# A hybrid decoder step on one core: the eight buffers of four moving rows get places at multiples of 512 bytes

## Chip, core and metric

The kernel runs on one core of a Trainium2 chip. The metric is the device time of one execution in microseconds (us); lower is better. The text speaks of TensorE (the matrix engine, PE in the profile, with PEld for its weight loads), VectorE (DVE), ScalarE (ACT), GpSimd (POOL) and the DMA queue of SyncE (SP). SBUF is the on-chip memory in which an operand's row lies in each of 128 partitions, PSUM the one that TensorE writes.

## What is computed

One decoder layer, for a prompt of 256 tokens and 8 samples of 4 tokens (288 tokens together), D = 2048, feed-forward width 8192, all in float32:

```python
h = rms_norm(x, norm1)
z = h @ w_in                       # all projections at once
q, k = partial_rope(...)           # sliding-window attention, 16 heads, sinks
o_swa, swa_state = swa_fn(q, k, v, sink)
log_a = log_sigmoid(ag @ w_a2 + b_a) / 16
o_g, S_new = gla_recurrent(q_g * 256**-0.5, k_g, v_g, log_a, S0)   # 4 heads, 256 x 512 states
o_g = rms_norm_per_head(o_g) * silu(rg)
y = sigmoid(gs) * (o_swa @ p_swa) + sigmoid(gg) * (o_g @ p_gla)
x = x + y @ w_o
h2 = rms_norm(x, norm2)
x = x + square(relu(h2 @ w_up)) @ w_down
```

Outputs are the final norm of x, the attention caches and the recurrent states.

## The kernel before

Activations lie transposed: a *row* k is one tile of 128 features by 288 tokens, so D = 2048 makes 16 rows. Every large product runs through `gemm` (L231): it streams one group of weights, 512 output features wide, in chunks (L234). A chunk is 512 KB of weights for two rows of k; ScalarE copies each half to `whi` (L227) and VectorE writes the rest of the precision to `wlo` (L228). For each row k and each of four slices m of 128 output features, three matmuls follow one another into the same bank of PSUM (L257 to L261): `whi` with the row's high part, `whi` with its low part, `wlo` with its high part. The weights are the stationary operand, the row of 288 columns is the moving one. A chunk has 2 x 4 x 3 = 24 matmuls, a gemm of 8 chunks has 192, and the 520 chunks have 12,480. At the end of a gemm the four banks are read out by `evac`, and the next gemm needs them empty again, bank after bank (`pmm` has four of them).

The order of the gemms is written out by hand (`ORDER`, L78): input projections (kv, q, gs, qk, v, gg, rg) with the attention projections ps among them, then pg0 to pg3, wo0 to wo3, and four blocks of up (four gemms) and dn (four gemms). Up to rg1 the attention and the linear attention are slipped between the chunks (`pump`, L211), with small matmuls of their own. From rg1 on TensorE runs gemm after gemm, up to the last one (dn3_3), with nothing between; VectorE does the states of the samples beside them (L1055).

The rows of a gemm come from these tiles. `rows` (L188) makes tiles of n rows that are 320 columns apart (1280 bytes), of which 288 are used; tiles whose name begins with hl, yl, ul, gl or h2l, all low parts, start 16 columns (64 bytes) into their buffer:

- `hh`, `yh`, `uh` (buffer XH) and `hl`, `yl`, `ul` (buffer XL): 16 rows each, for the input projections, wo and dn.
- eight buffers of four rows, Za0 to Za3 and Zb0 to Zb3, 5120 bytes each. For pg, row k is row k % 4 of `gh[k // 4]` and `gl[k // 4]`: gh0 to gh3 lie in Za0, Za2, Za3, Za1 (L991), gl0 to gl3 in Zb0 to Zb3 (L1013). For up, `h2h[j]` lies in Za j and `h2l[j]` in Zb j (L1034, L1035). So rows 12 to 15, that is chunks 6 and 7 of each of these gemms, use Zb3 for the low part, in pg beside Za1 and in up beside Za3.
- earlier the same eight buffers hold other tiles of the attention and linear attention, among them `kx1` (Zb3), `pt` and `kc` (Zb2, Za3), `e` (Za2, Za3), and at the end `kept` (all eight), which small matmuls read.

A pool gives each named buffer (tag) its place when a tile of that name is first asked for, one behind another, each as large as the largest tile of that name. XH, XL, Za2, Za1 and Zb1, the ten buffers of `whi` and `wlo`, come out at multiples of 512 bytes. Then come rs_m, the small nf, YA, zr and tt, and behind them Zb3, rs_t, Zb2, Za3, Za0, Zb0, sr, acc and rso.

Of the kernel before, what the change touches and what calls it, by code (L numbers as in the profile page):

```python
# [12 lines left out]
F32 = mybir.dt.float32  # L13
F32R = mybir.dt.float32r
# [5 lines left out]
P = 128  # L20
# [122 lines left out]
def step_kernel(ctx: ExitStack, tc: tile.TileContext, a: dict):  # L143
    nc = tc.nc
    V, S, G, T, SY = nc.vector, nc.scalar, nc.gpsimd, nc.tensor, nc.sync
    main = ctx.enter_context(tc.tile_pool(name="main", bufs=1))
# [38 lines left out]
    def big(tag, name, dt=F32, n=KT):  # L185
        return main.tile([P, n, NT], dt, name=name, tag=tag)

    def rows(tag, name, n=KT):  # L188

        off = 16 * name.startswith(("hl", "yl", "ul", "gl", "h2l"))  # L190
        return main.tile([P, n, 320], F32R, name=name, tag=tag)[:, :, off:off + NT]
# [116 lines left out]

    xa = big("SG", "x")
    hh, hl = rows("XH", "hh"), rows("XL", "hl")  # L310
    xn = []

    def x_row(k):
# [939 lines left out]
def build(arrays):  # L1253
    nc = bacc.Bacc("TRN2", target_bir_lowering=False, num_devices=1)
    aps = {}
    for n, v in arrays.items():
        aps[n] = nc.dram_tensor(f"in_{n}", v.shape, mybir.dt.from_np(v.dtype), kind="ExternalInput").ap()
    for n, s in OUTS.items():
        aps[n] = nc.dram_tensor(f"out_{n}", s, F32, kind="ExternalOutput").ap()
    with tile.TileContext(nc) as tc:  # L1260
        step_kernel(tc, aps)
    return nc
# [22 lines left out]
```

## Time and profile before

| | us |
|---|---|
| median of 3 runs | 1727.1 |
| lowest and highest of the runs | 1720.6 and 1727.28 |
| the profiled execution | 1727.3 |
| its span, first to last instruction | 1725.6 |
| TensorE busy in it | 1718.5 |
| VectorE busy | 1231.2 |
| ScalarE busy | 885.0 |

All times of the trace below are of the profiled execution, in us from the start of its span. The profile gives a matmul a duration that reaches into the next ones, because matmuls are pipelined; how long TensorE takes for each is read from the distance of their starts, or from the time that a stretch with a known number of them takes.

### The profile page before, as it was taken

The page shows a single profiled execution, that of the slowest core. Times are in us where ns is not written, and L with a number is a line of the kernel's source. Part 1 is how long each engine was busy: PE and PEld are TensorE (multiplying, and loading weights), DVE is VectorE, ACT ScalarE, POOL GpSimd, SP SyncE. Part 2 cuts the span into 40 slices and gives each one's busy share as a digit, 9 for nine tenths or more (in the row PEclk, how much of TensorE's full clock was granted, in tenths as well). Part 3 has the DMA queues.
Part 4 walks back from the last instruction along what each step waited for, and adds up shares of the span by engine and source line. Part 5 has one row for each costly group of instructions (what it writes and reads, how often), then busy time and mean ns, then how long its engine had stood idle before and what let it go on. Part 6 is the DMA issues. An engine that isn't in the chain of part 4 may idle for free.

```text
span 1725.6 us, 34513 instructions
## 1 busy us (share of the span) xinstructions
PE 1718.5 (100%) x13331; PEld 1691.6 (98%) x13331; DVE 1231.2 (71%) x2408; ACT 885.0 (51%) x1679; POOL 3.1 (0%) x12
## 2 busy tenths in 40 slices
PE   9999999999999999999999999999999999999998
PEld 8999999999999999999999999999999999999998
DVE  8885676857757576666778777677777777767554
ACT  7675464534544555544555554455445554445543
POOL 0000000000000000000000000000000000000000
PEclk9999999999999999999999999999999999999999
DMA  8778576676775655547657777866777687676753
GB/s 296 213 221 287 183 224 252 198 239 208 225 255 187 208 196 184 178 159 279 221 207 263 261 244 272 279 227 238 281 262 259 217 276 277 240 267 222 258 165 117
DMA packets 131701, 398.81 MB, mean 231 GB/s; under 512 B 21360, under 2 KB 39728, under 8 KB 127440
## 3 DMA queue, kind: packets, MB, share of 16 engines
q1 hardware_dynamic: 130096, 393.98, 67.2%
q10 hardware_dynamic: 1440, 2.62, 0.4%
q8 instruction: 104, 1.70, 0.4%
q14 instruction: 61, 0.50, 0.1%
HBM read 360.73 MB, written 35.82 MB: 230 GB/s over the span
## 4 chain that ended last, share of the span: by engine, by line
PE 99%; DMA 0%; DVE 0%; ACT 0%; issue 0%
PE mm L260 95%; PE pos L914 1%; PE mm L1180 1%; PE score L477 0%; PE o L520 0%; PE po L839 0%; DMA raw<-in_w 0%; PE po L842 0%; PE pa L767 0%; PE os L602 0%; PE scs L563 0%; PE ag L372 0%; PE po L841 0%; PE ssq L269 0%; PE pa L780 0%; PE pa L775 0%
## 5 line engine op out<-in xcount | busy, mean ns | idle before, releaser
L227 ACT CAST whi<-raw 128x512 fp32r<-128x512 f32 x1040 | 630.5, 618 | 714.4 <-PE mm L260 640.6
L167 DVE TENSOR_TENSOR wlo<-raw,whi 128x512 fp32r<-128x512 f32 x1040 | 702.3, 687 | 406.8 <-ACT whi L227 402.8
L260 PE MATMUL mm<-hh,whi 128*128 128x288 f32 x1472 | 433.9, 296 | 0.2 <-ACT whi L227 0.2
L260 PE MATMUL mm<-hl,whi 128*128 128x288 f32 x1472 | 431.2, 294 | 0.0
L260 PE MATMUL mm<-hh,wlo 128*128 128x288 f32 x1472 | 429.1, 292 | 0.0
L260 PE MATMUL mm<-h2l,whi 128*128 128x288 f32 x1024 | 302.2, 295 | 0.0
L260 PE MATMUL mm<-h2h,whi 128*128 128x288 f32 x1024 | 301.4, 294 | 0.0
L260 PE MATMUL mm<-h2h,wlo 128*128 128x288 f32 x1024 | 301.2, 294 | 0.0
L260 PE MATMUL mm<-uh,whi 128*128 128x288 f32 x1024 | 301.1, 294 | 0.0
L260 PE MATMUL mm<-ul,whi 128*128 128x288 f32 x1024 | 301.1, 294 | 0.0
L260 PE MATMUL mm<-uh,wlo 128*128 128x288 f32 x1024 | 300.7, 294 | 0.0
L260 PEld LDWEIGHTS mm<-hh,whi 128*128 128x128 f32 x1472 | 276.1, 188 | 6.5 <-ACT whi L227 3.7
L260 PEld LDWEIGHTS mm<-hh,wlo 128*128 128x128 f32 x1472 | 276.0, 188 | 0.1
L260 PEld LDWEIGHTS mm<-hl,whi 128*128 128x128 f32 x1472 | 275.9, 188 | 0.0
L260 PEld LDWEIGHTS mm<-h2h,wlo 128*128 128x128 f32 x1024 | 193.4, 189 | 0.0
L260 PEld LDWEIGHTS mm<-uh,wlo 128*128 128x128 f32 x1024 | 193.2, 189 | 0.0
L260 PEld LDWEIGHTS mm<-uh,whi 128*128 128x128 f32 x1024 | 192.4, 188 | 0.0
L260 PEld LDWEIGHTS mm<-h2h,whi 128*128 128x128 f32 x1024 | 192.4, 188 | 0.0
L260 PEld LDWEIGHTS mm<-h2l,whi 128*128 128x128 f32 x1024 | 191.9, 187 | 0.0
L260 PEld LDWEIGHTS mm<-ul,whi 128*128 128x128 f32 x1024 | 191.8, 187 | 0.0
L1073 DVE SCALAR_TENSOR_TENSOR acc_s<-vb,kdk,acc_s 128x512 f32<-128x512 f32 x192 | 142.4, 745 | 0.3
L260 PE MATMUL mm<-yl,whi 128*128 128x288 f32 x256 | 75.1, 294 | 0.0
(260 smaller groups left out, 1740.6 us busy)
## 6 DMA issues: line engine op xcount, KB each, us to landing
raw<-in_w SPq DMA_DIRECT2D x518, 512.0 KB, 4.3
vb<-vd SPq DMA_DIRECT2D x32, 1024.0 KB, 6.7
raw<-in_s SPq DMA_DIRECT2D x32, 512.0 KB, 4.6
old<-in_s SPq DMA_DIRECT2D x32, 512.0 KB, 4.9
out_ssn<-old SPq DMA_DIRECT2D x32, 512.0 KB, 4.6
pd<-tb SPq DMA_DIRECT2D x32, 96.0 KB, 2.1
pt<-pd SPq DMA_DIRECT2D x8, 384.0 KB, 4.7
kept<-kept SPq DMA_DIRECT2D x6, 512.0 KB, 5.9
```

The costliest lines, as they stand in the source:

```text
L167: eng.tensor_tensor(out, x, y, ALU.subtract)
L227: S.copy(hi, raw)
L260: T.matmul(o, lhsT=(lo if j == 2 else hi)[:, sl], rhs=xl(k) if j == 1 else xh(k), start=k == 0 and j == 0, stop=k == nk - 1 and j == 2)
L914: T.matmul(pos[r:r + 32], lhsT=qm[:, t, 32 * b:32 * b + 32], rhs=st[i + g][:, 512 * t:512 * t + 512], start=b < 2, stop=b >= NB - 2)
L1073: paced(V.scalar_tensor_tensor(acc[t], v(n), k(n), acc[t], ALU.mult, ALU.add))
L1180: mm = T.matmul(pst, lhsT=k[:, blk, P * t:P * t + P], rhs=v[:, blk], start=i == 0, stop=i == 5)
```

## The change

Right behind `hh` and `hl` a loop asks the pool for one tile of each of ten names, which nothing writes or reads. The sizes are those that the names have anyway.

```diff
     xa = big("SG", "x")
     hh, hl = rows("XH", "hh"), rows("XL", "hl")
+    for tag in ("Za2", "Za1", "Zb1", "whi", "wlo", "Zb3", "Zb2", "Za3", "Za0", "Zb0"):
+        if tag[0] == "Z":
+            main.tile([P, 4, 320], F32, name="place", tag=tag)
+        else:
+            main.tile([P, 512], F32R, name="place", tag=tag, bufs=5)
+
     xn = []
```

The order of places becomes Za2, Za1, Zb1, whi, wlo (as before), and then Zb3, Zb2, Za3, Za0, Zb0, ahead of rs_m. What each place is past a multiple of 512 bytes, worked out from the sizes in that order:

| buffer | before | after | its rows' starts before, past a multiple of 512 | after |
|---|---|---|---|---|
| Za1, Za2 | 0 | 0 | 0, 256, 0, 256 | the same |
| Zb1 (low part, 64 further on) | 0 | 0 | 64, 320, 64, 320 | the same |
| Za0, Za3 | 256 | 0 | 256, 0, 256, 0 | 0, 256, 0, 256 |
| Zb0, Zb2 (low part) | 256 | 0 | 320, 64, 320, 64 | 64, 320, 64, 320 |
| Zb3 (low part) | 128 | 0 | 192, 448, 192, 448 | 64, 320, 64, 320 |

rs_m, nf, YA, zr, tt and rs_t move by whole multiples of 512 bytes; all else in the pool, and the other pools, stay where they are, since the sum of the sizes is the same.

## Rows read from the trace of the kernel before

**Rows 1.** The page: span, TensorE's busy time (share, instructions), and the last chain by engine.
```profile
span 1725.6 us, 34513 instructions
...
PE 1718.5 (100%) x13331; PEld 1691.6 (98%) x13331; DVE 1231.2 (71%) x2408; ACT 885.0 (51%) x1679; POOL 3.1 (0%) x12
...
PE 99%; DMA 0%; DVE 0%; ACT 0%; issue 0%
```
**Rows 2.** Who TensorE waited for, whole span: us in total, times, longest.
```profile
PE mm L260 <- ACT whi L227: 0.2, 1, 0.2
PE ssq L269 <- DVE acc L164: 0.2, 1, 0.2
```
**Rows 3.** L260 by groups: busy us, mean ns of one, idle before.
```profile
L260 PE MATMUL mm<-h2l,whi 128*128 128x288 f32 x1024 | 302.2, 295 | 0.0
L260 PE MATMUL mm<-ul,whi 128*128 128x288 f32 x1024 | 301.1, 294 | 0.0
```
**Rows 4.** L260 by stretches, a gemm each: gg3, pg2, wo3, up0_1, dn0_1; window, length, busy, clock.
```profile
558.63:583.94 25.31, 25.31 (x194) 1.00 0.60 182
...
743.90:769.07 25.17, 25.17 (x195) 1.00 0.52 168
...
869.76:894.94 25.18, 25.18 (x195) 1.00 0.62 211
...
920.37:945.81 25.44, 25.44 (x195) 1.00 0.81 283
...
1022.00:1047.32 25.32, 25.32 (x194) 1.00 0.75 251
```
**Rows 5.** Timeline, TensorE: first matmul of each chunk of up0_1 and of up0_2's first.
```profile
920.37 0.29 PE L260 MATMUL mm<-h2h,whi 128*128 128x288 f32 x1
...
923.53 0.29 PE L260 MATMUL mm<-h2h,whi 128*128 128x288 f32 x1
...
926.69 0.30 PE L260 MATMUL mm<-h2h,whi 128*128 128x288 f32 x1
...
929.86 0.29 PE L260 MATMUL mm<-h2h,whi 128*128 128x288 f32 x1
...
933.03 0.29 PE L260 MATMUL mm<-h2h,whi 128*128 128x288 f32 x1
...
936.19 0.30 PE L260 MATMUL mm<-h2h,whi 128*128 128x288 f32 x1
...
939.35 0.29 PE L260 MATMUL mm<-h2h,whi 128*128 128x288 f32 x1
...
942.58 0.29 PE L260 MATMUL mm<-h2h,whi 128*128 128x288 f32 x1
...
945.81 0.29 PE L260 MATMUL mm<-h2h,whi 128*128 128x288 f32 x1
```
**Rows 6.** The same for chunks 6 and 7 of pg2 and the first of pg3.
```profile
762.78 0.29 PE L260 MATMUL mm<-gh,whi 128*128 128x288 f32 x1
...
765.92 0.29 PE L260 MATMUL mm<-gh,whi 128*128 128x288 f32 x1
...
769.07 0.29 PE L260 MATMUL mm<-gh,whi 128*128 128x288 f32 x1
```
**Rows 7.** Timeline where wo2 meets wo3, and wo3 meets up0_0: banks read out; up0_0's thirteenth matmul.
```profile
870.61 0.81 DVE L164 TENSOR_TENSOR x<-mm,x 128x288 f32<-128x288 f32 x2
...
895.89 0.81 DVE L164 TENSOR_TENSOR x<-mm,x 128x288 f32<-128x288 f32 x2
...
896.51 0.29 PE L260 MATMUL mm<-h2h,whi 128*128 128x288 f32 x1
```
**Rows 8.** Groups by line and shape: small matmuls that read the moved buffers.
```profile
L477 PE MATMUL score<-kx,qx 128*128 128x256 f32 x32 | 7.2, 306 | 0.0
...
L477 PE MATMUL score<-kx,qx 128*128 128x128 f32 x32 | 5.4, 249 | 0.0
...
L1180 PE MATMUL mm<-kept 128*128 128x512 f32 x24 | 5.9, 401 | 0.0
```

## Prediction

> **What bounds the kernel now.** I read the page first, then who TensorE waited for, then the pace of its matmuls, gemm by gemm and chunk by chunk. The page settles the engine: TensorE is busy for 1718.5 of 1725.6 us and 99% of the last chain is its own work [rows 1]. The waits show that it waits for almost nobody: two entries of 0.2 us [rows 2]. So no earlier transfer and no faster copy can bring time; only the pace at which matmuls follow one another can, and it is the only thing that a new place in SBUF could touch. The mean durations don't show that pace (294 and 295 ns for groups that differ in it, because durations overlap [rows 3]). Stretches of exactly one gemm, 192 matmuls, do: pg2 and wo3 take 25.17 and 25.18 us, dn0_1 25.32, up0_1 25.44 [rows 4], that is 131.1, 131.9 and 132.5 ns a matmul, all at the full granted clock (1.00). Two different things lie in these three figures.
>
> The first is a **rhythm**. pg2 and wo3 run at 25.17, dn0_1 at 25.32, although wo and dn read the same two buffers, XH and XL. gg3, on these buffers too, takes 25.31 [rows 4]. So the longer rhythm of dn, 0.14 to 0.15 us a gemm more, is no matter of where the rows lie; TensorE falls into it and stays. I went through the 12,480 starts in order of time: from the middle of rg1 to the end of wo3 every chunk has the short rhythm, and from up0_0 to the end every one the long.
>
> The second is **place**. Inside up0_1 the chunks begin at 920.37, 923.53, 926.69, 929.86, 933.03, 936.19, 939.35, 942.58 and 945.81 [rows 5]: the first six take 18.98 us together, 3.163 each, the last two 3.23 each. These two are rows 12 to 15, the only ones with the low part in Zb3, whose rows start 192 or 448 bytes past a multiple of 512. Chunks 0, 1, 4 and 5 use buffers at 256 past (Za0, Zb0, Zb2), chunks 2 and 3 buffers at 0, and they don't differ: 3.16 to 3.17 all. So an odd 256 costs nothing, the odd 128 of Zb3 0.067 us a chunk, 2.8 ns a matmul. All sixteen up gemms show the same jump at chunk 6.
>
> **The change, part by part.** (1) *The tiles named place* are not written or read: no instruction, no DMA, no wait is added or moved, on SP's queue or any other. The ring of five `whi` and five `wlo` buffers may start one further on; all ten lie at multiples of 512 bytes and each gemm uses all of them. Cost 0.
>
> (2) *Zb3 moves from 128 past to 0*, its rows to 64 and 320 past, which is where the rows of XL, Zb0, Zb1 and Zb2 start. I expect chunks 6 and 7 of an up gemm to take 3.163 us as chunks 0 to 5 do. The sum: 2 chunks x 0.067 us x 16 gemms = 2.1 us [rows 5]. The other way to it: up0_1 against dn0_1 in the same rhythm, 25.44 - 25.32 = 0.12 us, x 16 = 1.9 us [rows 4]. I take 2.0 us. All of it is on the path, because TensorE has nothing else in these stretches and the wait list has no L260 entry there [rows 2]. What is late next is nothing: VectorE and ScalarE have room (71% and 51% busy [rows 1]), and 2.0 us spread over 700 asks nothing more of them.
>
> (3) *pg reads Zb3 as well*, chunks 6 and 7 of four gemms. There it costs nothing now: pg2's chunks 6 and 7 take 3.14 and 3.15 us [rows 6], as an average chunk at 25.17 / 8 = 3.146 does. Nothing is to be gained. This is the one row that speaks against a plain rule "128 past costs": either the price is due in the long rhythm alone, or it needs the high part of Za3 beside Zb3, where pg has Za1. In both readings up's chunks 6 and 7 become like the others, because after the change Za3 and Zb3 lie as Za1 and Zb1 do.
>
> (4) *Za0, Za3, Zb0 and Zb2 move from 256 to 0.* By rows 5 that is worth 0.
>
> (5) *Small matmuls that read moved buffers.* `kx1` in Zb3 is the moving operand of half the 64 score matmuls, and `kept` is read by 24 matmuls and, with other tiles, 12 more at the end [rows 8]. Priced at what Zb3 costs a gemm's matmul, 2.8 ns, for 32 + 36 of them: 0.2 us at most, either sign; I take 0.
>
> (6) *rs_m, nf, YA, zr, tt and rs_t* move by whole multiples of 512, for VectorE, ScalarE and the DMA queues. The trace has no row of a duration that hangs on such a move; between wo (VectorE adds into x1, YA idle for it) and dn (states from YA) the matmuls' pace shows nothing of these engines beside the rhythm. 0.
>
> Sum: the profiled execution's 1727.3 - 2.0 = 1725.3 us. That execution stands 0.2 us above the median of the runs shown, so against the median the result would be 1725.1; I give 1725.3.
>
> [...]
>
> **Rivals.** *A, the long rhythm isn't entered.* It begins within up0_0, and one place there is tight. VectorE reads out banks 2 and 3 of wo3 from 895.89 on, 0.81 us for both; up0_0's thirteenth matmul, the first into bank 2, starts at 896.51, some 0.2 us behind the end of the first of the two. One gemm earlier the pair starts at 870.61, and the matmul that needs the bank follows at 869.76 + 12 x 0.131 = 871.33, some 0.1 us more room [rows 4, 7]. I read it so that the bank came a few ns late and that this slip threw TensorE from one rhythm into the other. If the slip fails to come, 32 gemms take 25.17 instead of 25.32, 0.14 to 0.15 us each, 4.6 us, and the 2.0 us of Zb3 are saved too: 1727.3 - 6.6 = 1720.7. The lowest run shown, 1720.6, is just there, so it seems to happen to the kernel as it is: by pg, the short rhythm has no price for Zb3, so that without the slip the old place and the new give the same 1720.7. For A: nothing in the margin is wide, and the change could set another beat upstream. Against: the order of VectorE's work is the same, and the median of the runs is that of a slip. Chance 0.22.
>
> *B, the change doesn't do what it says*: the price hangs on something that stays, such as which buffers pair up or what the last two chunks do besides. Against it: dn's last chunks have the same order and loads without the jump (its whole gemm, 25.32, is eight chunks of 3.165). 1727.3, chance 0.06. [...]
>
> *C, slower: the long rhythm rules earlier.* What decides is how TensorE comes out of the last of the slipped-in matmuls, in rg0 and rg1 near 618 us. Before, it came out short and stayed so for some eleven gemms up to 894.94. If it comes out long, these cost 11 x 0.14 = 1.5 us and leave a gain of 0.5. If the gemms before that, where breaks come every few chunks, run long as well, all the 33 gemms' worth ahead of up0_0 cost up to 33 x 0.14 = 4.6 us: 1725.3 + 4.6 = 1729.9. It is slower than before once more than 2.0 / 0.14 = 14 of them do. For it: gg3 shows that the long rhythm occurs there [rows 4]. Against: the breaks reset it, and nothing that the change moves decides it. Chance 0.08.
>
> **How the numbers follow.** Forecast 0.62 (1725.3, own range 1724.6 to 1726.0 from the two sums and the 0.2 us of the small matmuls), A 0.22 (1720.7), B 0.06 (1727.3), C 0.08 (1726.8 to 1729.9), 0.02 for what I don't see. A range for 8 in 10 has to reach from A to B; with 0.9 us below A and 0.7 above B for what separate executions differ by, 1719.8 to 1728.0. A difference under 0.5%, 8.6 us, can't be told from no change in a measurement of this kernel. No case reaches that: A is 0.38% faster, C at most 0.15% slower. So within 0.5%: 0.94, and 0.03 to each side for an unseen cause.
>
> **What would show it.** Right: in the up gemms all chunk distances are 3.16 to 3.17 us, an up gemm takes 25.31 to 25.33 us in the long rhythm (or 25.17 in the short), no longer 25.44; pg stays at 25.17; no new wait of L260. Wrong: chunks 6 and 7 still at 3.23 (B); a different distance in chunks 0, 1, 4 or 5, which would mean that an odd 256 matters after all. A shows as 25.17 in up and dn; C as 25.31 in rg2 to wo3. The forecast would fail in sign only if gemms ahead of up0_0 turned long for the most part, or if something that is not in these rows gave TensorE a new wait.

## The result

| | before | after |
|---|---|---|
| median of 20 runs each, us | 1727.0 | 1720.9 |
| lowest and highest | 1720.4 and 1727.6 | 1720.5 and 1725.4 |
| profiled execution (its span) | 1727.3 (1725.6) | 1720.8 (1719.0) |

The ratio of after to before is 0.9974, 95% interval 0.9965 to 0.9982 (it goes by all the single times, like the ratio of their means; the two medians stand at 0.9965). So after is faster, by less than 0.5%. The measured time lies 4.4 us below the forecast of 1725.3; it is that of rival A, 1720.7.

The medians hide what the single times show. Those of before lie in two groups with nothing between: 16 of 20 around 1727.1 (1726.7 to 1727.6) and 4 around 1720.8. Those of after lie in two groups as well: 18 of 20 around 1720.9 and 2 at 1725.0 and 1725.4. Every profiled execution in this study whose time is in a lower group runs up and dn in the short rhythm, every one in an upper group in the long one (or, in one kernel, in a variant of it). So I call the groups by the rhythm from here on, also where there is only a time.

The page of after, the lines that answer to [rows 1], and all that TensorE waited for, as in [rows 2]:

```profile
span 1719.0 us, 34513 instructions
...
PE 1711.6 (100%) x13331; PEld 1684.8 (98%) x13331; DVE 1230.4 (72%) x2408; ACT 884.5 (51%) x1679; POOL 3.1 (0%) x12
...
PE warm L405 <- DVE warm L399: 1.1, 1, 1.1
PE mm L260 <- ACT whi L227: 0.5, 1, 0.5
PE ssq L269 <- DVE acc L164: 0.2, 1, 0.2
```

The first of these waits, at the start of the kernel, is in before as well (1.1 us), though [rows 2] leave it out. The instructions are the same in number, TensorE is busy throughout as before, and there is no new wait. The span is 6.6 us shorter and TensorE's busy time 6.9 us (the wait for `whi` grew from 0.2 to 0.5 us): the gain is its pace alone. Stretches of one gemm in after (gg3, pg2, wo3, up0_0, up0_1, dn0_1, dn3_1; window, length, TensorE busy with its count, clock), against [rows 4]:

```profile
558.59:583.90 25.31, 25.31 (x194) 1.00 0.60 180
743.87:769.04 25.17, 25.17 (x195) 1.00 0.50 168
869.73:894.90 25.17, 25.17 (x194) 1.00 0.61 210
894.90:920.08 25.18, 25.18 (x194) 1.00 0.59 209
920.08:945.26 25.18, 25.18 (x195) 1.00 0.82 294
1020.78:1045.95 25.17, 25.17 (x194) 1.00 0.72 252
1624.94:1650.11 25.17, 25.17 (x194) 1.00 0.52 168
```

gg3 has its long rhythm as before, pg2 and wo3 their short one. up0_1 fell from 25.44 to 25.18 and dn0_1 from 25.32 to 25.17, although dn reads no buffer that was moved. Sixteen times 0.26 and sixteen times 0.15 make 6.6 us, the whole difference of the spans. Inside up0_1 the jump at chunk 6 of [rows 5] is gone. Before and after, chunks 0 to 5 and chunks 6 and 7 of up0_1, as windows of L260:

```profile
920.37:939.35 18.98, 18.98 (x146) 1.00 0.82 283
939.35:945.81 6.46, 6.46 (x51) 1.00 0.77 282
```
```profile
920.08:938.96 18.88, 18.88 (x146) 1.00 0.90 332
938.96:945.26 6.30, 6.30 (x51) 1.00 0.57 179
```

### The profile page after: what moved, and what is told of

Same layout as the page of the kernel before. It is cut to its first block, busy times and chain, and to the rows that moved or that the text cites. A ratio compares the mean times of both kernels' runs of the same rounds, so it can differ in the third digit from the quotient of the medians.

```text
span 1719.0 us, 34513 instructions
## 1 busy us (share of the span) xinstructions
PE 1711.6 (100%) x13331; PEld 1684.8 (98%) x13331; DVE 1230.4 (72%) x2408; ACT 884.5 (51%) x1679; POOL 3.1 (0%) x12
## 4 chain that ended last, share of the span: by engine, by line
PE 99%; DMA 1%; DVE 0%; ACT 0%; issue 0%; SPq 0%
PE mm L260 95%; PE pos L920 1%; PE mm L1186 1%; DMA raw<-in_w 1%; PE score L483 0%; PE o L526 0%; PE po L845 0%; PE po L848 0%; PE pa L773 0%; PE os L608 0%; PE scs L569 0%; PE ag L378 0%; PE po L847 0%; PE ssq L269 0%; PE pa L786 0%; PE pa L781 0%
## 5 line engine op out<-in xcount | busy, mean ns | idle before, releaser
L260 PE MATMUL mm<-hh,whi 128*128 128x288 f32 x1472 | 433.5, 295 | 0.5 <-ACT whi L227 0.5
L260 PE MATMUL mm<-hl,whi 128*128 128x288 f32 x1472 | 431.2, 294 | 0.0
L260 PE MATMUL mm<-hh,wlo 128*128 128x288 f32 x1472 | 429.2, 292 | 0.1
L260 PE MATMUL mm<-ul,whi 128*128 128x288 f32 x1024 | 300.6, 294 | 0.0
L260 PE MATMUL mm<-h2l,whi 128*128 128x288 f32 x1024 | 300.6, 294 | 0.0
L260 PE MATMUL mm<-h2h,whi 128*128 128x288 f32 x1024 | 300.4, 293 | 0.0
L260 PE MATMUL mm<-uh,whi 128*128 128x288 f32 x1024 | 300.4, 293 | 0.0
L260 PE MATMUL mm<-h2h,wlo 128*128 128x288 f32 x1024 | 298.7, 292 | 0.0
L260 PE MATMUL mm<-uh,wlo 128*128 128x288 f32 x1024 | 298.7, 292 | 0.0
L260 PEld LDWEIGHTS mm<-hh,whi 128*128 128x128 f32 x1472 | 275.8, 188 | 6.5 <-ACT whi L227 3.3
L260 PEld LDWEIGHTS mm<-hh,wlo 128*128 128x128 f32 x1472 | 276.1, 188 | 0.4 <-DVE wlo L167 0.3
L260 PEld LDWEIGHTS mm<-hl,whi 128*128 128x128 f32 x1472 | 275.7, 188 | 0.0
L260 PEld LDWEIGHTS mm<-uh,wlo 128*128 128x128 f32 x1024 | 192.2, 188 | 0.0
L260 PEld LDWEIGHTS mm<-h2h,wlo 128*128 128x128 f32 x1024 | 192.2, 188 | 0.0
L260 PEld LDWEIGHTS mm<-uh,whi 128*128 128x128 f32 x1024 | 192.0, 187 | 0.0
L260 PEld LDWEIGHTS mm<-h2h,whi 128*128 128x128 f32 x1024 | 192.0, 187 | 0.0
L260 PEld LDWEIGHTS mm<-h2l,whi 128*128 128x128 f32 x1024 | 192.0, 187 | 0.0
L260 PEld LDWEIGHTS mm<-ul,whi 128*128 128x128 f32 x1024 | 192.0, 187 | 0.0
L260 PE MATMUL mm<-gl,whi 128*128 128x288 f32 x256 | 75.1, 294 | 0.0
```

Source lines behind the costliest of these rows:

```text
L260: T.matmul(o, lhsT=(lo if j == 2 else hi)[:, sl], rhs=xl(k) if j == 1 else xh(k), start=k == 0 and j == 0, stop=k == nk - 1 and j == 2)
```

## The experiments

In each, the kernel before ran beside it on the same chip. The share of long executions of before was not the same each time: 16 of 20 in the first comparison, 10 of 35 beside the first four kernels below, 25 of 35 beside the next four, 13 of 15 beside the last four (these three on three different chips); in all four the short ones have a median of 1720.7 to 1720.9, the long ones of 1727.0 to 1727.2. So a ratio to before says little here, and I read the groups. (For the same reason before had a median of 1721.1 beside the first four, while it was 1726.9 to 1727.0 in the other comparisons.)

**Which rows matter, those of pg or those of up.** Two one-line edits of the kernel before move the low rows in Zb3 by 64 bytes, in pg alone or in up alone.

```diff
         off = 16 * name.startswith(("hl", "yl", "ul", "gl", "h2l"))
+        if name == "gl3":
+            off = 0
```

> The kernel before, with gl3 alone (pg's low rows 12 to 15, in Zb3) started 64 bytes earlier, at 128 and 384 past a multiple of 512 instead of 192 and 448; h2l3 in up stays at 192 and 448. Theory 'beat': the rows of Zb3 in pg cost no time but shift TensorE's beat of nine matmuls, and the beat decides whether the late bank at the meeting of wo3 and up0_0 throws it into the long rhythm; with gl3 out of the way it stays in the short one, where h2l3 costs nothing: 1720.8 us. Rival 'rows of up': the old place of h2l3 brings or holds the long rhythm: 1727.1. Rival 'other four buffers' (their move from 256 past to 0 did it): 1727.1.

8 of 12 short, median 1720.9; 4 long, 1727.5. Windows of pg2, wo3, up0_1 and dn0_1 of the profiled one:

```profile
743.51:768.74 25.23, 25.23 (x194) 1.00 0.51 168
869.49:894.66 25.17, 25.17 (x194) 1.00 0.61 210
919.86:945.03 25.17, 25.17 (x194) 1.00 0.84 291
1020.55:1045.73 25.18, 25.18 (x194) 1.00 0.72 251
```

The edit put gl3 into a place that isn't good either: pg2 takes 25.23 instead of 25.17. up0_1 is at 25.17 although h2l3 still starts at 192 and 448: in the short rhythm this place costs nothing. With a third of long ones, as beside it in the kernel before (10 of 35), this run tells nothing on the share.

The other edit has `h2l3` in place of `gl3`.

> The kernel before, with h2l3 alone (up's low rows 12 to 15) started 64 bytes earlier, at 128 and 384 past a multiple of 512; gl3 in pg stays. Theory 'beat': the long rhythm from up0_0 on stays (4.5 us), the price of chunks 6 and 7 of the up gemms goes (2.0 us): 1725.1 us, up gemms at 25.32. Rival 'rows of up': the long rhythm goes as well: 1720.8. A third outcome, that 128 past a multiple of 512 is as bad a start as 192: 1727.1, up gemms at 25.44.

All 12 executions long, 1724.4 to 1726.1, median 1725.4. Windows of pg2 and wo3, then up0_0 and up0_1, each parted in chunks 0 to 5 and chunks 6 and 7, then dn0_1:

```profile
743.86:769.04 25.18, 25.18 (x195) 1.00 0.53 168
869.73:894.90 25.17, 25.17 (x194) 1.00 0.61 210
...
894.90:913.80 18.90, 18.90 (x146) 1.00 0.55 167
913.80:920.18 6.38, 6.38 (x50) 1.00 0.90 337
920.18:939.16 18.98, 18.98 (x146) 1.00 0.89 328
939.16:945.51 6.35, 6.35 (x50) 1.00 0.55 177
...
1021.50:1046.82 25.32, 25.32 (x195) 1.00 0.73 250
```

The time is the 1725.1 that the beat theory gave, but not for its reason. The first six chunks of up0_0 are short (18.90); the long rhythm begins at chunk 6, which is h2l3, and stays. So here rows at 128 and 384 past a multiple of 512 themselves throw TensorE into the long rhythm, by the times in every execution (where it begins is seen in the profiled one alone). They have almost no price once it is there (6.35 against 6.46). The third outcome that I had written down, as bad as before, is wrong too: the starts 192 and 448 cost in the long rhythm and do not bring it about (they didn't in the profiled execution above), 128 and 384 bring it about and hardly cost.

**The beat.** The trace has starts in ns, and in the short rhythm the distances of nine successive starts repeat. Worked out from the starts, for matmuls 129 to 164 of pg1 (Zb3 is read from number 144 on) and the first 27 of up0_0:

```
before pg1   132 133 130 131 126 135 130 137 126 132 133 130 131 126 135 | 130 132 131 131 131 131 131 132 131 130 132 131 131 131 131 131 132 131 130 132 131
after  pg1   131 127 134 131 137 125 133 132 130 131 127 134 131 137 125 | 133 132 130 131 127 134 131 137 125 133 132 130 131 127 134 131 137 125 133 132 130
before up0_0 132 133 130 131 126 134 131 137 126 132 133 132 133 131 130 127 132 134 132 129 132 136 134 130 128 131 135
after  up0_0 131 127 134 131 136 126 133 132 130 131 127 129 133 133 136 134 131 133 131 126 135 130 137 126 132 133 130
```

In rg2 both kernels stand at the same place of the nine. In pg the rows of Zb3 run through another pattern of the same length in before (the sum of nine is 1180 ns in both), and come out displaced; so up0_0 begins with another of the nine. In both a disturbance follows at the thirteenth matmul, the first into bank 2: by the pattern it would start 130 ns behind the twelfth in before and 134 in after, and it starts 132 and 129 behind it. After it before goes on in the long pattern, after returns to the short one. My theory was that the position of the nine decides which. Matmuls that nobody needs, put in behind pg3, move the position:

```diff
         gemm(f"pg{j}", ...)
+    beat = bank("beat")
+    for i in range(3):
+        T.matmul(beat[:, :NT], lhsT=yh[:, 0, 0:P], rhs=(yl if i % 3 == 1 else yh)[:, 0], start=True, stop=True)
```

> The kernel before, all places as they were, with three matmuls more (yh and yl rows, into a bank that nobody reads) between pg3 and wo0: they cost 0.39 us and put the beat of nine on by three, to where it stands in the changed kernel. Theory 'beat': short rhythm through up and dn, no price for Zb3: 1721.2 us. Rivals that hold the places themselves to be the cause: 1727.1 + 0.4 = 1727.5.

10 of 12 long, median of these 1727.6; 2 short, 1721.4. The starts of the profiled execution show that up0_0 does begin at the position of the changed kernel, so the theory in this plain form, by which all would have been short, is wrong. The profiled execution is one of the two short ones; up0_1 (chunks 0 to 5, chunks 6 and 7) and dn0_1 in it:

```profile
920.82:939.71 18.89, 18.89 (x147) 1.00 0.87 312
939.71:946.00 6.29, 6.29 (x51) 1.00 0.67 230
...
1021.51:1046.69 25.18, 25.18 (x194) 1.00 0.72 252
```

All places are those of before, and chunks 6 and 7 take 6.29: no price in the short rhythm, shown here for up itself.

The changed kernel with `range(6)`:

> The changed kernel with six matmuls more between pg3 and wo0 (0.79 us), which put the beat of nine to where it stands in the kernel before. Theory 'beat': long rhythm from up0_0 on with all rows in good places, 1720.9 + 0.8 + 4.5 = 1726.2 us, up and dn gemms both at 25.32. Rivals that hold the places themselves to be the cause: 1721.7, up and dn at 25.17.

8 of 12 short, median 1721.8; 4 long, 1726.3. The usual time is the one that the rivals gave; the theory has only the long ones right. The profiled one is long, and up0_1 (parted as above) and dn0_1 in it read:

```profile
921.23:940.22 18.99, 18.99 (x146) 1.00 0.88 324
940.22:946.55 6.33, 6.33 (x50) 1.00 0.57 181
...
1022.50:1047.81 25.31, 25.31 (x194) 1.00 0.71 251
```

This is the long rhythm with all rows in the new places: 6.33 for chunks 6 and 7 is a third of 18.99. So 6.46 in before holds the price of Zb3's place, 0.13 us a gemm, 2.1 us for sixteen.

**The late bank.** In the kernel before, two sums of squares of wo3 are put behind the other two, so that VectorE reads out banks 2 and 3 sooner; nothing is left out.

```diff
+    held = []
     def wo_evac(j):
         def evac(m, ps):
             ...
+            if j == 3 and m < 2:
+                held.append(i)
+                return
             square_sum(acc2, x1[:, i], i == 0)
+            if m == 3:
+                while held:
+                    square_sum(acc2, x1[:, held.pop(0)], False)
```

> The kernel before, all places as they were; only VectorE's and ScalarE's order in wo3 is changed: the sums of squares of its first two slices come after those of the other two, so that bank 2 is read out some 0.9 us earlier and up0_0's thirteenth matmul does not wait for it. Theory 'late bank': without the slip the long rhythm is never entered, and in the short one Zb3 at 128 past a multiple of 512 costs nothing: 1720.7 us in every execution, none at 1727, up and dn gemms at 25.17. Rival 'place': TensorE falls into the long rhythm at Zb3's rows in some executions all the same: a mixture of 1720.7 and 1727.

12 of 12 short, 1720.4 to 1721.3, median 1720.6, while 25 of 35 executions of before beside it were long. VectorE in this kernel, and then in after, where wo3 meets up0_0, with up0_0's thirteenth matmul behind it (start, us, engine, line, operation):

```profile
894.32 0.45 DVE L164 TENSOR_TENSOR x<-mm,x 128x288 f32<-128x288 f32 x1
...
895.11 0.45 DVE L164 TENSOR_TENSOR x<-mm,x 128x288 f32<-128x288 f32 x1
...
896.22 0.29 PE L260 MATMUL mm<-h2h,whi 128*128 128x288 f32 x1
```
```profile
895.48 0.46 DVE L164 TENSOR_TENSOR acc<-acc,sq 128x288 f32<-128x288 f32 x1
895.86 0.81 DVE L164 TENSOR_TENSOR x<-mm,x 128x288 f32<-128x288 f32 x2
...
896.47 0.29 PE L260 MATMUL mm<-h2h,whi 128*128 128x288 f32 x1
```

The two reads of banks 2 and 3 start at 894.32 and 895.11 here, ahead of the thirteenth matmul of up0_0 by 1.9 and 1.1 us (it starts at 896.22). In after they start at 895.86, as in before [rows 7], for a matmul that starts at 896.47. The distances of the starts of up0_0 go on undisturbed in this kernel, and the gemm takes 25.18. So the late bank is what lets TensorE into the long rhythm in before; the old place of Zb3 by itself does not. It also means that after isn't rid of it: the bank is late there too. (It isn't the only way in: with `h2l3` moved TensorE was back in the short rhythm behind the late bank, 18.90 for chunks 0 to 5 of up0_0, and went long at chunk 6.) That the matmul waits for the bank is a reading: the read of bank 2 ends 0.17 us before the matmul starts in before and 0.16 us in after, and the list of waits has no entry there. The size of this gap doesn't tell the rhythms apart: in the profiled executions with the usual order it is 166 or 167 ns in the three that go long behind it and 156 to 169 in the nine that don't.

**Zb3 or the other four buffers.**

```diff
-    for tag in (..., "wlo", "Zb3", "Zb2", "Za3", "Za0", "Zb0"):
+    for tag in (..., "wlo", "Zb2", "Za3", "Za0", "Zb0"):
```

> Za0, Za3, Zb0, Zb2 at multiples of 512, Zb3 left at 128 past one. Theory 'late bank and beat': executions lie at 1720.8 (short) and 1727.1 (long, with the price of Zb3), the long share being that of the kernel before or not, since it hangs on few ns; the long ones cost 1727.1 because Zb3 has its price there. Rival 'the 256 matters': the long ones lie at another time than 1727.1.

6 of 12 long, median 1727.0; 6 short, 1720.8: both groups where before has them. The move of the four buffers from 256 to 0 is worth nothing in either rhythm. The price of Zb3 is there in the long one although Za3 beside it now lies at a multiple of 512. With Zb3 alone in the list behind `wlo`:

> Zb3 alone at a multiple of 512, the other four at 256 past one as before. Theory: executions lie at 1720.8 (short) and 1725.1 (long, no price left), none at 1727; if the beat that pg's Zb3 rows set decides the share of long ones, few are long, as in the changed kernel. Rival 'the other four': as before, 1727.1 in the long ones.

12 of 12 short, 1720.5 to 1721.4, median 1720.7. Zb3 alone does what the whole change does, and by the starts it is what moves the position too: up0_0 begins where it does in before when the four others are moved, and where it does in after in this run. And the changed kernel once more, on this chip:

> The changed kernel once more, beside the kernel before on this chip. Theory 'places decide the share of long executions': before mostly 1727, this mostly 1720.9 again, as in the first comparison. Theory 'the share hangs on the chip and the moment': both kernels have like shares, the long ones at 1727.1 before and at 1725.1 here, and the medians stand no farther apart than 2 us when both are long, and not apart when both are short.

12 of 12 short, median 1720.9, ratio 0.9972 (0.9960 to 0.9983), where before was long in 25 of 35: here the shares go with the kernels and not with the chip and the moment. With the first comparison, 2 of 44 executions with Zb3 at a multiple of 512 were long, and of those of before and of the kernel with the four others 47 of 67 in the same two comparisons.

**Position against place.** Three more runs set the two against each other.

> The kernel before, places as they were, with six matmuls more between pg3 and wo0 (0.79 us): the third position of the beat of nine. Short executions 1721.5, long ones 1727.9. Theory 'place': Zb3 at 128 past, so half or more are long, as in the kernel before (and with three more, 10 of 12). Theory 'beat': the share belongs to the position, so it is that of the changed kernel with three more matmuls, run beside this.

5 of 5 short, 1721.5. Theory 'place' in this form is wrong: before was long in 13 of 15 beside it.

> The changed kernel with three matmuls more between pg3 and wo0 (0.39 us): the third position of the beat, with Zb3 at a multiple of 512. Short executions 1721.3, long ones 1725.6. Theory 'place': few long, at most a third. Theory 'beat': the same share as the kernel before with six more.

5 of 5 short, 1721.2, which both theories allow.

> The changed kernel with nine matmuls more between pg3 and wo0 (1.18 us): the beat stands where it stands in the changed kernel itself. Short executions 1722.1, long ones 1726.4. Theory 'beat' and theory 'place' both: hardly any long (2 of 32 so far without the nine). If a third or more are long, the added matmuls themselves raise the share, and the third of long ones with six more says nothing on the beat.

7 of 11 long, median of these 1726.6; 4 short, 1722.1. Neither theory had this, and by what was written down the 4 of 12 with six more say nothing on the beat.

| position of the nine at up0_0 | Zb3 at 128 past | Zb3 at a multiple of 512 |
|---|---|---|
| that of before | before 64 of 105 long; four others 6 of 12; gl3 moved 4 of 12; h2l3 moved 12 of 12 | after + 6 matmuls: 4 of 12 |
| that of after, no matmul added | | after and Zb3 alone: 2 of 44 |
| that of after, matmuls added | before + 3: 10 of 12 | after + 9: 7 of 11 |
| the third | before + 6: 0 of 5 | after + 3: 0 of 5 |

The position is read from one profiled execution of each kernel, and the lines mix comparisons. Before + 3 and after + 6 ran where before was long in 10 of 35, after + 9 and the third position where it was in 13 of 15, and the changed kernel without added matmuls ran in neither. Within a comparison the added matmuls move the share a good deal with all places as they are: in the first of these two, before went from 10 of 35 to 10 of 12 with three; in the other it went from 13 of 15 to 0 of 5 with six, and the changed kernel had 0 of 5 with three and 7 of 11 with nine. That they do it by the position is argued, not shown: the second and third line have one position and 2 of 44 against 17 of 23, so the added matmuls change something else as well, or the chip or the moment does. Whether the old and the new place of up's rows differ in the share at one position isn't settled by these few executions either; that rows of up can decide it is shown by h2l3 at 128 and 384. What else decides it, no run shows.

**Without the late bank, in the changed kernel.**

> The changed kernel with the order of the sums of squares in wo3 of the fifth run, so that bank 2 is read out early: no slip at the meeting of wo3 and up0_0. Theory 'late bank': every execution short, 1720.7 us, none at 1725; against the changed kernel's own median no gain (1720.9), only its rare long executions gone.

5 of 5 short, 1720.6 to 1721.2, median 1720.8. It is no faster than the changed kernel's usual execution, and the same as the kernel before with this order (1720.6): where the late bank is gone, the change of places is worth nothing that can be measured. As the changed kernel is nearly always short anyway, its 5 of 5 add little; the starts of up0_0 go on undisturbed here too.

## Why the prediction was right and where it failed

**What was right.** TensorE's pace is the only thing that changed. *The price of Zb3*: 2.0 us were forecast for part (2); the long executions fell from 1727.1 to 1725.2, by 1.9 (after has only two of them), and the profiled long one with six matmuls more has chunks 6 and 7 at 6.33 instead of 6.46. The two readings left open in part (3) are settled: the price is due in the long rhythm alone, for up0_1 has 6.29 with three matmuls more and the places of before; and it doesn't need Za3's old place, for with the four others moved, Za3 among them, the long executions stand at 1727.0. *The four other buffers*: 0 in part (4), and 1720.8 and 1727.0 in the run that moves these four alone. *Rival A's number*: 1720.7 against 1720.9, and its remark that in the short rhythm the old place and the new come to the same time: 1720.8 and 1720.9 in the first comparison.

**The step that failed** is the one between the forecast and rival A. I took the long rhythm as given, with 0.62 against 0.22, because the one trace had it and two of the three times shown looked like it, and because the order of VectorE's work stays. The share was 16 of 20 before, 2 of 20 after: the change moved the share, and with it the median from one group to the other. That put the time 4.4 us below the sum's 1725.3. That it lies within the stated range is owed to A, to which the range was drawn down, and not to the sum; and that the median of before lay in the long group is luck too, for beside the first four experiments it was 1721.1. In part (3) I wrote that pg's rows have nothing to give, since they cost nothing; they cost nothing (pg2 takes 25.17 before and after), but they displace the beat with which TensorE arrives at up0_0. That the move of Zb3 alone took the share down is shown (0 of 12, against 6 of 12 with the four others moved and Zb3 left). That it did so by pg's rows is argued from the starts, not shown: no run put only pg's rows into a good place. The prediction also said that a difference under 0.5% can't be told from none; this one, with 0.9965 to 0.9982, can.

**The mechanism of rival A was half right.** The bank that comes late is the door into the long rhythm here: with it out of the way 12 of 12 executions were short at the old place, where 25 of 35 were long beside them (at the new one 5 of 5). But I thought of the late bank as coming or not. It came in the changed kernel too (its read ends 0.16 us ahead of the matmul, in before 0.17); what differs is the rhythm in which TensorE settles behind it.

**Rivals B and C.** B falls with the price, above. C did not occur: gg3 and the gemms to wo3 take 25.31 and 25.17 before and after.

**What stays open.** What sets the share of long executions (that the position in the nine has a part is argued, and it isn't enough), and why that share of one and the same kernel was 29% beside some runs and 87% beside others: the chips differed, and no run tells the chip from the moment. Since before had its median at 1721.1 in one of four comparisons, the 6.1 us are what this change gave in the two in which both kernels ran, not a constant of the kernel. Where an execution is long in both, the change gives about 1.9 us; where it is short in both, nothing.

## What to carry to other kernels

Where one engine is busy all the time and its pace still differs between stretches of equal work, read the distances of its starts, and keep apart what a place costs and what decides the rhythm: a place may cost only in one rhythm (chunks 6 and 7 at Zb3's old place and at the new: 6.46 against 6.33 us in the long one, 6.29 against 6.30 in the short), and rows that hardly cost may decide which one comes (`h2l3` at 128 and 384: 6.35, and 12 of 12 long). Look at the single times before a median: two groups mean that a change can win by moving the share (from 16 of 20 long to 2 of 20), and such a gain has to be measured again beside other runs. The surer way here was not the place of a buffer but to read out two banks over 1 us sooner where two gemms meet (bank 2 at 894.32 instead of 895.89 in the kernel before, 12 of 12 executions short; 5 of 5 in the changed one).

## What the hardware showed that I had not expected

- At the full granted clock (1.00 throughout these gemms) a stream of matmuls of 288 columns, each with its own weights, has at least two rhythms, 131.1 ns (25.17 us for 192) and 131.9 ns (25.32), and keeps either for hundreds of us: in before the short one lasted from 618.15 to 894.94; the long one lasted from up0_0 through 256 chunks to the end, and it began behind one disturbance of a few ns in the distances (132 ns where the pattern had 130).
- Where the low part's rows start matters, though all these starts are multiples of 64 bytes: at 64 and 320 past a multiple of 512 no price was seen; at 192 and 448 none in the short rhythm and 0.13 us a gemm, in 48 of its matmuls, in the long one (6.46 against 6.33); at 128 and 384 0.06 us a gemm in the short one (pg2 25.23 against 25.17), and in up, by the times, TensorE was in the long one in 12 of 12 executions. A start 256 further on is worth nothing (1720.8 and 1727.0 with the four others moved).
